# Gate logits and first convolution taps on ScalarE, and a new price list for the issue order of a hybrid conformer block

## Chip, cores and metric

One core of a Trainium2 chip. The metric is the device time of one execution in microseconds; several runs of a kernel are summed up by their median.

## What is computed

One layer (DEPTH = 1) on x of 512 tokens x 1024 channels, all in float32:

```python
x = x + 0.5 * swiglu_ffn(rms_norm(x, ffn1_norm), ffn1_w13, ffn1_w2)      # D_FF = 2816
h = rms_norm(x, mix_norm)
a, g, q, k, v, fl = split(h @ w_in)              # 512, 512, 512, 512, 512, 8 columns
u = a * sigmoid(g)                               # group A: causal depthwise conv, width 31
y_conv = silu(layer_norm(conv(u, conv_w) + conv_b))
log_f = log_sigmoid(fl + forget_b)               # group B: 8 heads x 64, forgetting attention
D = cumsum(log_f)
p = softmax(q k^T / 8 + D[t] - D[s], causal)
y_attn = p @ v
y = concat(rms_norm(y_conv), rms_norm(y_attn))
x = x + y @ w_out
x = x + 0.5 * swiglu_ffn(rms_norm(x, ffn2_norm), ffn2_w13, ffn2_w2)
out = rms_norm(x, final_norm)
```

`fl` are the gate logits, one per head and token.

## The kernel before

Activations lie with channels on the 128 partitions and 512 tokens along the free dimension, in 8 tiles `xs[d]`. A product in float32 precision is made of three fast matmuls: both operands are split into a high part (`whi`, `xh`; a ScalarE cast to fp32r) and a low part (`wlo`, `xl`; what is left, by VectorE), and `product` issues hi x hi, hi x lo and lo x hi for each of the 8 k-steps. Weights come by DMA into `raw` (three buffers); `cast` makes `whi` on ScalarE and then `wlo` on VectorE (two buffers each). Products follow one another in the order of the program (`in_turn`).

The stages are feed-forward 1 (tiles `f1...`), the mixer, and feed-forward 2 (`f2...`). In the down projections of the feed-forward stages `seven` saves an eighth of the matmuls by sums of weight blocks, made on GpSimd and VectorE. The mixer goes through `ORDER`: `c0 c1 c2 v c3 a0 a1 n a2 a3 w0 w1 w2 w3`.

- `c`: `conv_tile(i)`, 128 of the 512 convolution channels. Products `pg` and `pa`, then `u = a * sigmoid(g)`, then 31 taps. For tiles 0 and 2 a tap is a ScalarE multiplication into `tap` (two buffers) and a GpSimd sum into `acc`; for tiles 1 and 3 (`DVE_CONV`) it is one VectorE instruction on `conv`, which lies in PSUM.
- `v`: `values()`, in two halves of 260 columns: 256 of `v` and 4 gate logits, into four banks `pv` of 128 tokens each. Each bank is drained by ScalarE (`vt`, scaled by the RMS factor `rcol`) and by VectorE (`zf`, 128x4, scaled by `rcol` plus the bias). Then a chain of small VectorE instructions makes log sigmoid (`lf`) from `zf`.
- `a`: `attention(i)`, two heads: products `pq` and `pk`; `gates` (only at a0) makes the cumulative sum, which goes through DRAM (`cumd`) and comes back spread over the partitions (`ck`). For each head and block of 128 queries: scores `s` on TensorE, `sm`/`mn` on VectorE (bias and row minimum), the exponential on ScalarE, transposes `pt` on TensorE, the copy `pT` on ScalarE, and the product `po`.
- `n`: `conv_norm`, layer norm and RMS norm of the four convolution tiles, which starts when their last taps are done and ends in `yh` and `yl`.
- `w`: the output projection `wo`; w0 and w1 take the convolution half.

The order of instructions on every engine is not the order of the program text. Each call on V, S, PE, G and Q (VectorE, ScalarE, TensorE, GpSimd, the SP DMA queue) is recorded in `Plan`. `price` gives each a duration, `schedule` builds a list schedule: each operation has a rank (its urgency plus the longest path of prices behind it); at each step every engine offers the ready operation that can start first (highest rank among equals), and the earliest of these is placed. Each engine then gets its instructions in that order, and on the chip an instruction waits at the head of its queue until what it needs is there. So prices do not change what is computed, only what stands behind what. The profile gives line 242 for all of them, the line that emits.

Of the kernel before, what the change touches and what calls it, by code (L numbers as in the profile page):

```python
# [36 lines left out]
P = 128  # L37
# [22 lines left out]
ORDER = "c0 c1 c2 v c3 a0 a1 n a2 a3 w0 w1 w2 w3"  # L60
# [14 lines left out]
SEM = 0.15  # L75
COPY, ACT = 0.05, 0.07
PENALTY = 40.0
URGENT_IN, URGENT_STATS, URGENT_V, URGENT_LF, URGENT_LN, URGENT_END = 20.0, 200.0, 200.0, 200.0, 200.0, 200.0
URGENT_Q, URGENT_OUT, URGENT, URGENT_X = 3.0, 3.0, 50.0, 50.0
# [66 lines left out]
class Buf:  # L146
    def __init__(self, make, dt, slots):
        self.make, self.dt, self.slots, self.tile = make, dt, slots, None
        self.uses, self.left = [], 0
# [14 lines left out]


class Plan:


    SEM, SAME = SEM, {"V": 0.13, "S": 0.1, "G": 0.13, "PE": 0.0, "Q": 0.0}
    SWITCH = 1.3  # L170

    def __init__(self, tc):
        self.tc, self.ops, self.tags, self.joined, self.urgency = tc, [], {}, None, 0.0

    def tile(self, pool, shape, dt, tag, name, bufs=1):
        slots = self.tags.setdefault((id(pool), tag), Slots(bufs))
        buf = Buf(lambda: pool.tile(shape, dt, tag=tag, name=name, bufs=bufs), dt, slots)
        slots.queue.append(buf)
        size = int(np.prod(shape))
# [24 lines left out]
    def record(self, engine, target, method, args, kwargs):  # L204
# [30 lines left out]
        cost, table = self.price(engine, method, args, kwargs, out)  # L235
# [10 lines left out]
    def price(self, engine, method, args, kwargs, out):  # L246
# [24 lines left out]

    def schedule(self):
# [15 lines left out]
        clock = dict.fromkeys(engines, 0.0)  # L288
        ready = {e: [] for e in engines}
# [936 lines left out]
```

## Time and profile before

| | |
|---|---|
| median of 3 runs (lowest to highest) | 946.19 us (945.72 to 946.75) |
| the profiled execution | 946.2 us, span 944.5 us |
| TensorE clock granted, mean | 0.998 |
| busy, share of the span: TensorE | 932.1 us, 99% |
| weight loads | 793.7 us, 84% |
| VectorE | 653.8 us, 69% |
| ScalarE | 433.7 us, 46% |
| GpSimd | 154.0 us, 16% |
| chain that ended last | TensorE 89%, VectorE 3%, GpSimd 3%, ScalarE 3% |
| DMA | 91.19 MB, mean 97 GB/s |

The span runs from the first to the last instruction. Busy shares are means over stages that differ; a TensorE bar covers a matmul with its pipeline, so neighbouring bars overlap and a short gap between two starts leaves no idle time in this table.

### The profile page before, as it was taken

Reading aid. Unit: us, or ns where it says so; the run is one execution under the profiler, and the core shown is the slowest. Engines: PE = TensorE matmul, PEld = TensorE weight load, DVE = VectorE, ACT = ScalarE, POOL = GpSimd, SP = SyncE. Lnnn points to the kernel's source line nnn. Section 1 sums busy time; section 2 is a strip of 40 time slices with the busy share of each in tenths; the row PEclk is TensorE's granted clock in tenths of the full one; section 3 lists DMA queues with packets and bytes.
Section 4 is the critical chain, followed back from the end, with each engine's and each line's share of the span. In section 5 each row is a group of like instructions: output and inputs, shape, how many; then the busy total and the mean of one; then the engine's idle time right before and its main releaser. Section 6 shows DMA issues by size and latency. Waiting matters only on the chain.

```text
span 944.5 us, 13463 instructions
## 1 busy us (share of the span) xinstructions
PE 932.1 (99%) x5277; PEld 793.7 (84%) x5277; DVE 653.8 (69%) x990; ACT 433.7 (46%) x679; POOL 154.0 (16%) x132
## 2 busy tenths in 40 slices
PE   9999999999999999999999999999999999999997
PEld 7888999888999888897677777888899888899887
DVE  6655887657776465798977766555777755876554
ACT  7433433334433245677869755333433333433344
POOL 1000211001112000999843000000121001111000
PEclk9999999999999999999999999999999999999999
DMA  7222323232432132223211122222332222332222
GB/s 247 91 91 94 130 90 112 70 109 69 138 116 99 51 110 92 90 90 112 90 68 46 67 67 88 91 90 92 116 128 90 90 89 90 112 112 97 66 84 90
DMA packets 34207, 91.19 MB, mean 97 GB/s; under 512 B 3544, under 2 KB 13912, under 8 KB 34144
## 3 DMA queue, kind: packets, MB, share of 16 engines
q1 hardware_dynamic: 33600, 90.13, 28.4%
q8 instruction: 41, 0.67, 0.3%
q10 hardware_dynamic: 544, 0.20, 0.1%
q14 instruction: 22, 0.18, 0.1%
HBM read 88.21 MB, written 2.11 MB: 96 GB/s over the span
## 4 chain that ended last, share of the span: by engine, by line
PE 89%; DVE 3%; POOL 3%; ACT 3%; issue 1%; DMA 1%; SPq 0%; DVEq 0%; POOLq 0%
PE f2g L242 13%; PE f2u L242 13%; PE f1g L242 13%; PE f1u L242 13%; PE f1p L242 9%; PE f2p L242 9%; PE wo L242 5%; PE f2o L242 4%; PE f1o L242 3%; POOL acc L242 3%; PE pg L242 1%; PE pq L242 1%; PE pa L242 1%; PE s L242 1%; PE po L242 1%
## 5 line engine op out<-in xcount | busy, mean ns | idle before, releaser
L242 ACT CAST whi<-raw 128x1024 fp32r<-128x1024 f32 (+3 forms) x152 | 150.6, 991 | 278.8 <-issue 132.0
L242 DVE TENSOR_TENSOR wlo<-raw,whi 128x1024 fp32r<-128x1024 f32 (+3 forms) x152 | 184.8, 1216 | 21.1 <-ACT whi L242 18.3
L242 POOL TENSOR_TENSOR acc<-acc,tap 128x512 f32<-128x512 f32 x60 | 90.0, 1500 | 80.7 <-ACT tap L242 74.2
L242 PE MATMUL f1u<-xh,whi 128*128 128x512 f32 x176 | 68.8, 391 | 0.6 <-ACT xh L242 0.6
L242 PE MATMUL f1u<-xl,whi 128*128 128x512 f32 x176 | 68.6, 390 | 0.3 <-DVE xl L242 0.3
L242 PE MATMUL f2g<-xh,whi 128*128 128x512 f32 x176 | 68.7, 390 | 0.0
L242 PE MATMUL f2g<-xl,whi 128*128 128x512 f32 x176 | 68.6, 390 | 0.0
L242 PE MATMUL f2u<-xh,whi 128*128 128x512 f32 x176 | 68.6, 390 | 0.0
L242 PE MATMUL f1u<-xh,wlo 128*128 128x512 f32 x176 | 68.5, 389 | 0.0
L242 PE MATMUL f2g<-xh,wlo 128*128 128x512 f32 x176 | 68.5, 389 | 0.0
L242 PE MATMUL f2u<-xl,whi 128*128 128x512 f32 x176 | 68.5, 389 | 0.0
L242 PE MATMUL f2u<-xh,wlo 128*128 128x512 f32 x176 | 68.5, 389 | 0.0
L242 PE MATMUL f1g<-xh,whi 128*128 128x512 f32 x168 | 65.8, 392 | 0.0
L242 PE MATMUL f1g<-xl,whi 128*128 128x512 f32 x168 | 65.5, 390 | 0.0
L242 PE MATMUL f1g<-xh,wlo 128*128 128x512 f32 x168 | 65.4, 389 | 0.0
L242 POOL TENSOR_TENSOR f2S<-raw 128x512 f32<-128x512 f32 x8 | 11.1, 1392 | 310.5 <-DMA raw<-w2b 294.9
L242 DVE TENSOR_TENSOR f2un<-f2u,rstd_f2in 128x512 f32<-128x512 f32 x22 | 15.2, 691 | 63.0 <-PE f2u L242 63.0
L242 DVE TENSOR_TENSOR f1un<-f1u,rstd_in 128x512 f32<-128x512 f32 x22 | 15.2, 690 | 54.8 <-PE f1u L242 54.8
L242 POOL TENSOR_TENSOR f1S<-raw 128x512 f32<-128x512 f32 x8 | 10.4, 1294 | 261.6 <-DMA raw<-w2a 227.0
L242 ACT ACTIVATE tap<-u,par 128x512 f32<-128x512 f32 x60 | 42.8, 720 | 20.9 <-POOL acc L242 20.6
L242 DVE SCALAR_TENSOR_TENSOR conv<-u,par,conv 128x512 f32<-128x512 f32 x60 | 45.1, 752 | 1.2
L242 PEld LDWEIGHTS f1u<-xh,whi 128*128 128x128 f32 x176 | 33.1, 188 | 8.1 <-ACT xh L242 1.1
(420 smaller groups left out, 2410.3 us busy)
## 6 DMA issues: line engine op xcount, KB each, us to landing
raw<-w13b SPq DMA_DIRECT2D x44, 512.0 KB, 3.4
raw<-w13a SPq DMA_DIRECT2D x42, 512.0 KB, 3.5
raw<-w2a SPq DMA_DIRECT2D x16, 512.0 KB, 3.6
raw<-w2b SPq DMA_DIRECT2D x16, 512.0 KB, 3.5
raw<-wag SPq DMA_DIRECT2D x8, 512.0 KB, 3.4
raw<-wqk SPq DMA_DIRECT2D x8, 512.0 KB, 3.4
raw<-wo SPq DMA_DIRECT2D x8, 512.0 KB, 3.4
raw<-w2a SPq DMA_DIRECT2D x16, 192.0 KB, 2.4
```

Of the source, the lines that this page charges most:

```text
L242: ins = getattr(target, method)(*real, **kw)
```

## The change

Three things are changed; arithmetic is the same apart from where it is done.

1. The gate logits are drained by ScalarE, as `rcol` times the four columns, into `p5`, a part of the PSUM tile `ps` that is now allocated at the head of `values`; one VectorE addition of the bias for all 8 heads and 4 blocks makes `zf`.
2. The first tap of convolution tiles 1 and 3 is a ScalarE activation (as it was for tiles 0 and 2), and VectorE adds the other 30.
3. The planner has new prices and rules. Prices by form, with PSUM operands told apart; latencies between engines by the engine that was waited for; ScalarE and VectorE may start 0.1 and 0.08 us before the last instruction ends; an operation with `port` (any on GpSimd, and on VectorE a two-operand one without PSUM) does not start while the other engine has one; a change of tile size on TensorE costs 0.1 or 0.17; a DMA costs its queue 0.1 and its transfer is counted on a common bus. `URGENT`, the urgency of attention, goes from 50 to 80.

`LATE` is False, so what depends on it is as before (`ORDER`, the places of `k` and `po`); `URGENT_W` is 0.0, which changes no rank.

```diff
-SEM = 0.15
-COPY, ACT = 0.05, 0.07
+SEM = {"V": 0.05, "S": 0.05, "G": 0.05, "PE": 0.2, "Q": 2.0}
+SAME = {"V": 0.03, "S": 0.02, "G": 0.06, "PE": 0.0, "Q": 0.0}
+OVERLAP = {"V": 0.08, "S": 0.1, "G": 0.0, "PE": 0.0, "Q": 0.0}
+TILED, UNTILED = 0.1, 0.17
-URGENT_Q, URGENT_OUT, URGENT, URGENT_X = 3.0, 3.0, 50.0, 50.0
+URGENT_Q, URGENT_OUT, URGENT, URGENT_X, URGENT_W = 3.0, 3.0, 80.0, 50.0, 0.0
...
-    SEM, SAME = SEM, {"V": 0.13, "S": 0.1, "G": 0.13, "PE": 0.0, "Q": 0.0}
-    SWITCH = 1.3
+    SEM, SWITCH = 0.15, 1.3
...
         if engine == "PE":
-            dt = args[1].buf.dt
-            passes = 4 if dt == F32 and method == "matmul" else 2 if dt == F32 else 1
-            part = args[1].at[0].size / P if method == "matmul" else 1
-            return 0.003 + n * passes / 2400.0 * max(part, 0.25), None
+            if method != "matmul":
+                return n * 0.00084, None
+            part = args[1].at[0].size / P
+            if args[1].buf.dt != F32:
+                return 0.0133 + n / 2400.0, None
+            if part > 0.5:
+                return 2 * max(0.02 + n * 0.00069, 0.1), None
+            op.tiled = part
+            return (0.13 if part > 0.3 else 0.084) * max(n, 64) / P, None
         if method == "dma_start" and engine != "Q":
             return 0.1, None
+        psum = any(isinstance(v, View) and v.buf.psum for v in list(args) + list(kwargs.values()))
         if engine == "S":
+            cost = (0.143 if psum else 0.2) + n * 0.00083
             if method == "copy":
-                return COPY + n * 0.00084, None
-            return ACT + n * 0.00084, None if args[2] in (AF.Copy, AF.Square, AF.Identity) else args[2]
+                return cost, None
+            if isinstance(kwargs.get("scale"), View) or isinstance(kwargs.get("bias"), View):
+                cost += 0.09
+            if "accum_out" in kwargs:
+                op.late = 0.1
+            return cost, None if args[2] in (AF.Copy, AF.Square, AF.Identity) else args[2]
         if engine == "G":
-            return 0.1 + n * (0.0024 if method.startswith("tensor_") else 0.0012), None
+            op.port = 1.0
+            return 0.1 + n * (0.00233 if method.startswith("tensor_") else 0.0008), None
         if engine == "Q":
-            return 0.1 + n * 4 * P / 330e3, None
+            op.bytes += n * 4 * P
+            return 0.1, None
         if method == "tensor_tensor_scan":
             return 0.06 + n * 0.0022, None
         if method == "reciprocal":
-            return 0.06 + n * 0.0064, None
+            return 0.15 + n * 0.0062, None
+        if method in ("tensor_copy", "tensor_scalar") and not psum:
+            return 0.15 + n * 0.0006, None
+        if not psum:
+            op.port = 1.0
         if method == "scalar_tensor_tensor":
-            return 0.06 + n * 0.00118, None
-        return 0.06 + n * 0.00108, None
+            return 0.15 + n * 0.00118, None
+        return 0.15 + n * 0.00105, None
...
             for o in op.before.values():
-                lat = self.SAME[op.engine] if o.engine == op.engine else self.SEM
-                if o.engine == "Q":
-                    lat = 2.0
-                t = max(t, o.end + lat)
+                t = max(t, o.end + (SAME if o.engine == op.engine else SEM)[o.engine])
...
                     t = max(t, clock[e])
+                    if op.port:
+                        t = max(t, port["G" if e == "V" else "V"])
...
-            op.start, op.end = t, t + cost
-            clock[e] = op.end
+            if e == "PE" and op.tiled != tiled:
+                cost += TILED if tiled == 1.0 else UNTILED
+                tiled = op.tiled
+            op.start, op.end = t, t + cost + op.late
+            clock[e] = t + cost - (0.0 if op.late else OVERLAP[e])
+            if op.port:
+                port[e] = t + cost - (0.1 if e == "G" else 0.0)
+            if e == "Q":
+
+                bus = op.end = max(bus, t) + op.bytes / 330e3
...
-            if i in DVE_CONV and j == 0:
-                V.tensor_scalar(a, u[:, 0:T], w, bias, ALU.mult, ALU.add)
-            elif i in DVE_CONV:
+            if i in DVE_CONV and j:
                 V.scalar_tensor_tensor(a, u[:, j:j + T], w, a, ALU.mult, ALU.add)
             elif j == 0:
                 S.activation(a, u[:, 0:T], AF.Identity, scale=w, bias=bias)
...
     def values():
+
+        ps = plan.tile(pp, [P, 16, NT, H], F32, "pt", "e", PT)
+        p1, p2, p3, p4, p5 = (ps[:, n] for n in range(5))
...
-                V.scalar_tensor_tensor(zf[:, t, 4 * c:4 * c + 4], pv[t][:, 4 * HD:VC], rc,
-                                       par[:, G_FB + 4 * c:G_FB + 4 * c + 4], ALU.mult, ALU.add)
+                S.activation(p5[:, t, 4 * c:4 * c + 4], pv[t][:, 4 * HD:VC], AF.Copy, scale=rc)
             plan.urgency = 0.0
...
         plan.urgency = URGENT_LF
+        V.tensor_add(zf, p5, par[:, G_FB:G_FB + H].over(NT))
         lf, e1, e2, e3 = (tile_([P, NT, H], n, n) for n in ("lf", "e1", "e2", "e3"))
-        ps = plan.tile(pp, [P, 16, NT, H], F32, "pt", "e", PT)
-        p1, p2, p3, p4 = (ps[:, n] for n in range(4))
```

## Rows read from the trace of the kernel before

**Rows 1.** Busy time by stage: stretch, its length, each engine's busy time (instructions), clock, DMA.
```profile
17.70:362.00 344.30, 344.30 (x1844) 298.23 (x1843) 235.55 (x341) 131.20 (x189) 24.32 (x25) 1.00 0.30 100
362.00:587.00 225.00, 221.04 (x1442) 175.51 (x1441) 176.83 (x286) 156.71 (x273) 105.52 (x76) 1.00 0.24 79
587.00:932.00 345.00, 345.00 (x1883) 301.19 (x1882) 225.15 (x331) 130.14 (x189) 21.59 (x16) 1.00 0.28 94
932.00:944.50 12.50, 6.02 (x50) 5.58 (x48) 6.37 (x16) 3.29 (x9) 0.00 (x0) 0.87 0.54 168
```

**Rows 2.** Chain of waits, a product of feed-forward 2: start, length, what.
```profile
591.76 5.44 PE f2g L242 x24
```

**Rows 3.** Timeline, TensorE in the mixer: start, length, what, [idle before, its releaser].
```profile
426.38 0.50 PE L242 MATMUL pa<-xh,wlo 128*128 128x512 f32 x1 [0.58 <-DVE wlo L242]
...
452.38 0.70 PE L242 MATMUL s<-k,q 128*128 128x256 f32 x2 [1.46 <-DVE mn L242]
...
455.18 0.91 PE L242 MATMUL s<-k,q 128*128 128x384 f32 x2 [0.74 <-DVE mn L242]
...
457.57 0.40 PE L242 MATMUL pk<-xh,wlo 128*128 128x512 f32 x1
458.07 0.33 PE L242 MATMUL pt<-ident,sm 128*128 128x128 f32 x1
...
511.99 0.50 PE L242 MATMUL wo<-yl,whi 128*128 128x512 f32 x1 [0.22 <-DVE yl L242]
...
514.66 0.44 PE L242 MATMUL pt<-ident,sm 128*128 128x128 f32 x2 [0.44 <-ACT pT L242]
```

**Rows 4.** Busy time, 390 to 456 us (order: PE, PEld, DVE, ACT, POOL).
```profile
390.00:456.00 66.00, 63.09 (x370) 54.23 (x368) 61.80 (x97) 47.22 (x71) 61.28 (x41) 1.00 0.30 98
```

**Rows 5.** Timeline of VectorE in the mixer, 406 to 455 us.
```profile
406.55 0.22 DVE L242 SCALAR_TENSOR_TENSOR zf<-pv,rcol,par 128x4 f32<-128x4 f32 x1
406.68 1.51 DVE L242 TENSOR_TENSOR wlo<-raw,whi 128x1040 fp32r<-128x1040 f32 x1
...
434.58 1.22 DVE L242 TENSOR_TENSOR wlo<-raw,whi 128x1024 fp32r<-128x1024 f32 x1 [1.17 <-ACT whi L242]
435.73 0.81 DVE L242 TENSOR_SCALAR conv<-u,par 128x512 f32<-128x512 f32 x1
...
448.43 3.12 DVE L242 SCALAR_TENSOR_TENSOR conv<-u,par,conv 128x512 f32<-128x512 f32 x4
451.45 0.68 DVE L242 SCALAR_TENSOR_TENSOR q<-pq,rstd_f1n 64x512 f32<-64x512 f32 x1
452.05 0.27 DVE L242 CUSTOM_DVE_ANT_0 sm<-s,ck 128x128 f32<-128x128 f32 x1
...
452.73 2.05 DVE L242 TENSOR_TENSOR wlo<-raw,whi 128x1024 fp32r<-128x1024 f32 x1 [0.19 <-ACT whi L242]
```

**Rows 6.** The tile `tap`: instructions with their min/median/max in ns; who idled for whom.
```profile
L242 ACT ACTIVATE tap<-u,par x60: 706/724/727, 377.2 to 478.0; 128x512 f32<-128x512 f32 x60
L242 POOL TENSOR_TENSOR acc<-acc,tap x60: 1267/1295/2308, 377.9 to 478.9; 128x512 f32<-128x512 f32 x60
...
  POOL acc L242: 20.6, 24
```

**Rows 7.** Timeline of ScalarE, its smallest activations in the mixer.
```profile
425.71 0.20 ACT L242 ACTIVATE e<-e 128x32 f32<-128x32 f32 x1
425.84 0.71 ACT L242 ACTIVATE tap<-u,par 128x512 f32<-128x512 f32 x1
```

**Rows 8.** Timelines of GpSimd and VectorE, the last convolution tap on each.
```profile
478.89 2.26 POOL L242 TENSOR_TENSOR acc<-acc,tap 128x512 f32<-128x512 f32 x1 [2.66 <-ACT pT L242]
...
482.69 0.75 DVE L242 SCALAR_TENSOR_TENSOR conv<-u,par,conv 128x512 f32<-128x512 f32 x1
```

**Rows 9.** Timeline of TensorE, a product going on behind a run of small matmuls.
```profile
528.51 0.50 PE L242 MATMUL wo<-yh,whi 128*128 128x512 f32 x1
528.84 0.40 PE L242 MATMUL wo<-yl,whi 128*128 128x512 f32 x1
```

More of the change, by code (lines that the diff above doesn't have):

```diff
@@ L56 @@
 BIG = 1e30
-ORDER = "c0 c1 c2 v c3 a0 a1 n a2 a3 w0 w1 w2 w3"
+LATE = False
+ORDER = "c0 c1 c2 v c3 a0 a1 n a2 a3 w0 w1 w2 w3" if not LATE else "c0 c1 c2 v c3 a0 a1 a2 n a3 w0 w1 w2 w3"
 EARLY = 2
@@ L148, in __init__ @@
         self.make, self.dt, self.slots, self.tile = make, dt, slots, None
-        self.uses, self.left = [], 0
+        self.uses, self.left, self.psum = [], 0, False
 class Slots:
@@ L163, in __init__ @@
         self.rank, self.waits, self.start, self.end, self.follows = 0.0, 0, 0.0, None, None
+        self.port, self.tiled, self.late, self.bytes = 0.0, 1.0, 0.0, 0
 class Plan:
-    SEM, SAME = SEM, {"V": 0.13, "S": 0.1, "G": 0.13, "PE": 0.0, "Q": 0.0}
-    SWITCH = 1.3
+    SEM, SWITCH = 0.15, 1.3
     def __init__(self, tc):
-        self.tc, self.ops, self.tags, self.joined, self.urgency = tc, [], {}, None, 0.0
+        self.tc, self.ops, self.tags, self.joined, self.urgency, self.psum = tc, [], {}, None, 0.0, None
     def tile(self, pool, shape, dt, tag, name, bufs=1):
@@ L178, in tile @@
         slots.queue.append(buf)
+        buf.psum = pool is self.psum
         size = int(np.prod(shape))
@@ L234, in record @@
                     op.bufs.append(v.buf)
-        cost, table = self.price(engine, method, args, kwargs, out)
+        cost, table = self.price(op, engine, method, args, kwargs, out)
         op.cost += cost
@@ L244, in record, with price @@
         op.emits.append(emit)
-    def price(self, engine, method, args, kwargs, out):
+    def price(self, op, engine, method, args, kwargs, out):
         n = out.n if isinstance(out, View) else 512
         if engine == "PE":
-            dt = args[1].buf.dt
-            passes = 4 if dt == F32 and method == "matmul" else 2 if dt == F32 else 1
-            part = args[1].at[0].size / P if method == "matmul" else 1
-            return 0.003 + n * passes / 2400.0 * max(part, 0.25), None
+            if method != "matmul":
[7 more added lines that the diff above has]
+            return (0.13 if part > 0.3 else 0.084) * max(n, 64) / P, None
         if method == "dma_start" and engine != "Q":
             return 0.1, None
+        psum = any(isinstance(v, View) and v.buf.psum for v in list(args) + list(kwargs.values()))
         if engine == "S":
+            cost = (0.143 if psum else 0.2) + n * 0.00083
             if method == "copy":
-                return COPY + n * 0.00084, None
-            return ACT + n * 0.00084, None if args[2] in (AF.Copy, AF.Square, AF.Identity) else args[2]
+                return cost, None
[4 more added lines that the diff above has]
+            return cost, None if args[2] in (AF.Copy, AF.Square, AF.Identity) else args[2]
         if engine == "G":
-            return 0.1 + n * (0.0024 if method.startswith("tensor_") else 0.0012), None
+            op.port = 1.0
+            return 0.1 + n * (0.00233 if method.startswith("tensor_") else 0.0008), None
         if engine == "Q":
-            return 0.1 + n * 4 * P / 330e3, None
+            op.bytes += n * 4 * P
+            return 0.1, None
         if method == "tensor_tensor_scan":
@@ L288, in schedule @@
         clock = dict.fromkeys(engines, 0.0)
+        port = {"V": 0.0, "G": 0.0}
+        tiled, bus = 1.0, 0.0
         ready = {e: [] for e in engines}
@@ L375, in block_kernel @@
     pp = ctx.enter_context(tc.tile_pool(name="pp", bufs=1, space=bass.MemoryType.PSUM))
+    plan.psum = pp
     dr = ctx.enter_context(tc.tile_pool(name="dr", bufs=1, space=bass.MemoryType.DRAM))
@@ L483, in unit @@
         lo = wide(shape, "wlo", f"wlo{n}", SPLITS, F32R)
-        return cast(hi, lo, raw)
+        with plan.urgent(URGENT_W):
+            return cast(hi, lo, raw)
     def load_and_split(i, raw, hi, lo, a, b):
@@ L1031, in attention @@
             if stacked:
-                h, l = (tile_([P, T], f"u{2 * b + n}", f"k{i}{b}{n}", 1, F32R) if i % 2 == 0 else
-                        slot(16 + 2 * b + n, f"k{i}{b}{n}", F32R) for n in range(2))
+                h, l = (tile_([P, T], f"u{2 * b + n}", f"k{i}{b}{n}", 1, F32R) if (i % 2 == 0) != LATE else
+                        slot((0 if LATE else 16) + 2 * b + n, f"k{i}{b}{n}", F32R) for n in range(2))
                 G.memset(f32(l)[other], 0.0)
@@ L1049, in attention @@
         sums = tile_([P, NT, 2], "sums", f"sums{i}", 2)
-        po = bank("misc", f"po{i}", MISC) if i == 0 else bank("cv", f"po{i}")
+        po = bank("misc", f"po{i}", MISC) if i < (3 if LATE else 1) else bank("cv", f"po{i}")
         quarters = []
```

## The prediction

> **What bounds the kernel now.** I read the stages first: the busy time of each engine in stretches of the span [rows 1]. TensorE has no idle time from 587 to 932 us, nor from 18 to 362, while the middle stretch, 362 to 587 (mixer: convolution, attention, output projection), has 225.0 us with 221.0 busy. The chain of waits shows how tight the feed-forward stages are: 24 product matmuls in 5.44 us, 0.227 us each, every time [rows 2]. Nothing that VectorE, ScalarE or GpSimd do faster can shorten those stages. What can be won lies in the middle, and a little at the two ends; TensorE's granted clock is full there.
>
> A busy TensorE hides short stalls: a matmul's bar lasts 0.39 us while the next one can start after 0.227, so 0.16 of each stall lies under a bar. In the middle the timeline shows idle time before five matmuls [rows 3], at 426.38, 452.38, 455.18, 511.99 and 514.66; with 0.16 added to each they are 0.74, 1.62, 0.90, 0.38 and 0.60. Four more lie wholly under bars and are found by the starts alone, as at 457.57, where the next one comes 0.50 later in place of 0.227; they are 0.24 to 0.29 each, 1.07 together. The sum of the nine is 5.3 us. That is all there is to win in the middle without changing TensorE's own work.
>
> The next view is who the stalled matmuls wait for. The three largest name VectorE (`wlo`, then `mn` twice). VectorE is busy 61.8 of the 66 us from 390 to 456, GpSimd 61.3, ScalarE only 47.2 [rows 4]. VectorE's timeline at the largest stall shows its queue: four convolution taps of 3.12 us, then `q`, then the `sm` whose `mn` frees the score bank [rows 5]. VectorE ran its list without a gap and was simply late. One reason is in the same view: the cast's second half `wlo` took 1.22 us with GpSimd out of its way and 2.05 beside a tap sum; the tap sum on GpSimd took 1.27 to 2.31, median 1.295 [rows 5, 6]. The old planner prices neither.
>
> **The change, part by part.** *VectorE gets lighter.* Two first taps leave, 0.81 us each, one of them at 435.73 [rows 5]: 1.6 us. Eight `zf` instructions leave; one is 0.22 us long but the next instruction starts 0.13 after it [rows 5], so 8 x 0.13 = 1.0 (1.7 at the full length). One add of 128x32 comes back, between 0.13 and 0.22. Net: 2.4 us off, 3.1 at most, all before 450 us, in the stretch where VectorE has 4.2 us of idle.
>
> *ScalarE gets heavier.* Two taps at 0.72 [rows 6], 1.3 to 1.4 us with the overlap of neighbours. Eight copies of four columns: no row shows one; the nearest is a 32-column `e` of 0.20 us [rows 7], so 0.1 (overlapped) to 0.2 each, I take 0.15, since the tap behind that `e` starts 0.13 after it: 1.2. Together 2.5 us (2.1 to 3.0) on an engine with 18.8 us idle in that stretch. What hides it is that idle; without that cover the cast `whi` behind the copies is late, then `wlo`, then the product that needs it, up to 1.6 us at the second group of gate columns.
>
> The Trainium skill, page ScalarE: Activation LUTs, section Rules for kernel authors, speaks against this move: it wants adds and multiplications on VectorE, not on ScalarE. No sentence of the sum uses it; here the f32 tap takes 0.72 on ScalarE and 0.81 on VectorE [rows 5, 6], so the trace does not agree for this form.
>
> *The order.* Nothing on TensorE is added or removed. The planner's price of a 512-column ScalarE tap rises from 0.50 to 0.72 (0.62 after overlap), which is what the row says [rows 6]; the price of three product matmuls from 0.65 to 0.68, as in the chain; a sum of two SBUF operands on VectorE and any GpSimd instruction are now planned one after the other. DMA issues no longer hold the queue for their transfer: in the plan small transfers (the row sums' detour through DRAM, `cumd` and `ck`) may go earlier, never behind a load's transfer; the real queue has the same waits for freed buffers as before. The wait that the change adds is one: `zf` now follows a ScalarE copy and one add. Queued behind that add on VectorE are convolution taps; who needs it (the transposes of `lf`) is over 5 us later behind a whole product, so I cost it at nothing, and at 0.4 us if that cover were gone.
>
> *What that is worth at the nine places.* At 452 and 455 (2.52): VectorE arrives 2.4 us earlier less what falls into its idle time; I take 2.0. At 426 (0.74): `wlo` has less ahead of it, but its `whi` now stands behind more on ScalarE; I take 0, with 0.74 and -1.6 as bounds. At 512 and 515 (0.98): the wait is for `yl`, the end of the chain that starts when the last convolution tap is done. The last tap on VectorE starts at 482.69, after GpSimd's last at 478.89 [rows 8], so a lighter VectorE brings this forward; I take half, 0.5. The four smaller ones (1.07): a better price of ScalarE helps them in general; 0.3, bounds 0 and 1.07. What is late next at 452 would be ScalarE's `sm` and the cast behind its taps, which is why I don't take all. Sum: 2.0 + 0 + 0.5 + 0.3 = 2.8.
>
> *Both ends.* From 932 on the order of small steps is replanned too; with the same operations I expect 0, bounds 0.5 either way. The head waits for transfers of x and weights, which do not change.
>
> The profiled execution has a span of 944.5 us and a time of 946.2, so 1.7 lie around the span; the median of the runs is 946.19, the same. Forecast: 946.2 - 2.8 = **943.4**.
>
> **Rivals.**
> 1. *More and smaller batches on TensorE.* Between 362 and 587 I count 53 runs of small matmuls (scores, transposes, sums) between product matmuls. After one, the first product matmul takes 0.33 us in place of 0.227, as at 528.51 [rows 9]; with the change into it I price a run at 0.1 to 0.2, 0.15 as a middle. The prices of switching lengthen the plan but choose nothing. With each score ready at its own time, and attention's urgency up from 50 to 80, runs may split: 16 more cost 2.4 us: 943.4 + 2.4 = 945.8, no change. For it: ScalarE is now planned slower, so pieces are ready further apart. Against: fewer late pieces also means fewer splits around a stall.
>    The Trainium skill, page TensorEngine Tiling (Array Packing), section Key Properties, says that a change of tiling mode drains TensorE. By it only the runs of 32 and 64 columns would pay; the 0.10 at 528.51, behind a 64-column run, agrees.
> 2. *ScalarE takes the place of VectorE.* Taps on ScalarE wait for GpSimd 24 times, 20.6 us in all [rows 6], and everything behind a waiting tap waits too. If the eight copies stand ahead of the casts between 410 and 430, the stall at 426 grows by up to 1.6, and 0.6 is lost at the next cast: 943.4 + 2.2 = 945.6. Against: ScalarE has 28% of the stretch idle.
> 3. *The convolution ends later: slower.* In the plan a tap sum and a `wlo` now stand apart: 1.295 + 1.22 = 2.52 us; overlapped the longer of the two needed 2.05 to 2.31 [rows 5, 6]. If the plan opens a gap on GpSimd for each of some 20 casts before 480 us, at 0.35 (2.52 less a middle of 2.17), the taps end 7.0 us later. GpSimd's last tap starts 3.8 us before VectorE's last but lasts 1.5 longer, so 2.3 are slack; beyond that the wait for `yl` at 512, which has no slack left, grows one for one: 4.7. With the 2.0 won at 452 and 455: 946.2 - 2.0 + 4.7 = 948.9. It is slower by more than the bound from about 18 such gaps. Against: 2.4 us come off VectorE, and a tap sum that waits in the plan waits on the chip as well.
>    The Trainium skill, page SBUF — State Buffer, section Who interferes with whom, says that the second of two such instructions blocks fully until the first is done. By it standing apart costs next to nothing and this rival is void; the 2.05 to 2.31 seen here lie just under the 2.52 of full blocking, so the trace leans to it.
> 4. *The order hardly changes* where it matters; then only the ten moved instructions count, half of the gain: 944.8.
>
> **How the numbers follow.** Forecast 0.58; rival 1 0.15; rival 2 0.10; rival 3 0.12; rival 4 0.05. About 0.2%, 1.9 us, is what a measurement of this kernel can tell from no change, so faster means under 944.3 and slower over 948.1: faster 0.58, same 0.15 + 0.10 + 0.05 = 0.30, slower 0.12. Low end: all nine places gone and 0.5 at the tail, 946.2 - 5.3 - 0.5 = 940.4. High end: it takes in rivals 1, 2 and 4 and the mild half of rival 3 (some 16 gaps): 946.2 - 2.0 + 16 x 0.35 - 2.3 = 947.5. What lies outside is about 1 in 10 above and less below, as the nine places limit the gain.
>
> **What would show it.** Right: busy TensorE from 362 to the start of the second feed-forward stage, with that stretch shorter by about 2.8 us; both feed-forward stages unchanged at 5.44 us per 24; VectorE under 60 us in the 66 from 390; no wait of a score matmul for `mn` over 0.5 us; eight ScalarE copies of 128x4 at 0.2 or less. Rival 1 shows as over 65 runs of small matmuls; rival 2 as TensorE waiting for `wlo` with `whi` just before it on ScalarE; rival 3 as the last tap after 486 us and a wait for `yl` of several us. The forecast is wrong if TensorE's idle time merely moves to other places in the middle, or if the head or the feed-forward stages show stalls that they do not have now.

## The result and the profile after

The changed kernel takes 949.23 us (median of 6 runs, 947.31 to 950.38), the kernel before 946.09 beside it (945.66 to 946.79): a ratio of 1.003, interval 1.002 to 1.004. It is **slower by 0.3%**, where 943.4 was forecast. The profiled execution of after took 949.7 us with a span of 947.9, so the tables of the two traces differ by 3.4 us of span.

The page of after, its span and busy times:

```profile
span 947.9 us, 13474 instructions
PE 933.5 (98%) x5277; PEld 796.3 (84%) x5277; DVE 653.1 (69%) x981; ACT 434.5 (46%) x688; POOL 154.6 (16%) x132
```

The stretches of after, with the columns of [rows 1] and [rows 4] (length, then busy us and instructions of PE, PEld, DVE, ACT and POOL, granted clock, DMA share, GB/s). The first and the last are the feed-forward stages:

```profile
17.70:362.00 344.30, 344.30 (x1845) 298.55 (x1845) 234.46 (x342) 131.18 (x188) 25.41 (x25) 1.00 0.30 100
390.00:456.00 66.00, 60.62 (x355) 53.21 (x354) 56.47 (x87) 43.95 (x75) 50.69 (x34) 0.97 0.29 97
...
587.00:932.00 345.00, 345.00 (x1875) 300.77 (x1872) 225.66 (x330) 130.94 (x188) 22.35 (x16) 1.00 0.28 94
```

The feed-forward stages have no idle time, as before. In the 66 us from 390, VectorE went from 61.8 to 56.5 us, as the change meant it to, though by more than the 2.4 us that were taken off it: over the whole span VectorE is busy 653.1 us where it was 653.8, so part of its work only stands later. GpSimd went from 61.3 to 50.7. But TensorE is busy for only 60.6 of these 66, and the granted clock has a mean of 0.97. All but 0.2 us of the loss lies in the middle: the second feed-forward stage begins its matmuls at 582.41 where it began at 579.13, 3.28 us later, and goes on at the pace of [rows 2]. The chain of before at that place, then the chain of after, its first and a later link there:

```profile
579.13 3.41 PE f2g L242 x15
```

```profile
582.41 4.08 PE f2g L248 x18
...
595.03 5.44 PE f2g L248 x24
```

What TensorE waited for from 362 to 587 in after, the first three (us in total, times, longest):

```profile
PE pv L248 <- DVE wlo L248: 4.4, 2, 3.0
PE s L248 <- DVE mn L248: 0.7, 2, 0.5
PE s L248 <- DVE k L248: 0.5, 1, 0.5
```

The wait of scores for `mn`, the largest before, went from 2.2 to 0.7, and those of `pa` for `wlo` and of `wo` for `yl` are not in the list any more [rows 3]. In their place stand two waits in the product of the values, where before only one matmul began late, by 0.2 us at 408.24. TensorE's timeline of after (start, length, idle before it and who ended it):

```profile
409.59 0.39 PE L248 MATMUL pv<-wlo,xh 128*128 128x260 f32 x1 [1.39 <-DVE wlo L248]
...
418.67 0.39 PE L248 MATMUL pv<-wlo,xh 128*128 128x260 f32 x1 [3.04 <-DVE wlo L248]
...
419.74 0.42 PE L248 MATMUL pv<-whi,xh 128*128 128x260 f32 x1
419.95 0.42 PE L248 MATMUL pv<-wlo,xh 128*128 128x260 f32 x1
```

With the part hidden under the bars, counted as for [rows 3] by the starts, they are 1.55 and 3.20 us: 4.75. And one microsecond after the second, the value matmuls go from 0.12 us apart to 0.215: TensorE has fallen to its lower level, 1.2 GHz, and stays there until 423.18. Its clock in that stretch (length, PE busy, granted clock, DMA share, GB/s):

```profile
415.60:418.60 3.00, 0.03 (x1) 1.00 0.00 0
419.80:423.00 3.20, 3.20 (x17) 0.50 0.36 140
```

3.4 us at half speed lose 1.7. **The account of the middle** is then as follows. The late starts (the times by which matmuls of the middle begin later than the pace allows, as summed for [rows 3]) are 5.36 us before and 7.38 after. Of the 7.38, 4.75 are new; the rest, 2.63, is 2.7 less than before, about the gain that was forecast (2.8). 7.38 - 5.36 + 1.7 = 3.7; the stretch is longer by 3.3, and the 0.4 between are about what three runs of small matmuls fewer (50 where there were 53) are worth at 0.1 each [rows 9].

**Why was `wlo` late?** Its first half was not: ScalarE's timeline of after ends the two `whi` at 405.00 and 410.67, 2.9 and 5.8 us before the `wlo` made from them begins.

```profile
403.96 1.04 ACT L248 CAST whi<-raw 128x1040 fp32r<-128x1040 f32 x1
...
409.61 1.06 ACT L248 CAST whi<-raw 128x1040 fp32r<-128x1040 f32 x1
```

VectorE's timeline of after shows what it did with those microseconds:

```profile
402.51 5.49 DVE L248 SCALAR_TENSOR_TENSOR conv<-u,par,conv 128x512 f32<-128x512 f32 x7
407.91 1.62 DVE L248 TENSOR_TENSOR wlo<-raw,whi 128x1040 fp32r<-128x1040 f32 x1
409.46 7.08 DVE L248 SCALAR_TENSOR_TENSOR conv<-u,par,conv 128x512 f32<-128x512 f32 x9
416.45 2.17 DVE L248 TENSOR_TENSOR wlo<-raw,whi 128x1040 fp32r<-128x1040 f32 x1
418.54 3.12 DVE L248 SCALAR_TENSOR_TENSOR conv<-u,par,conv 128x512 f32<-128x512 f32 x4
...
427.34 0.19 DVE L248 TENSOR_TENSOR zf<-e,par 128x32 f32<-128x32 f32 x1 [4.56 <-ACT e L248]
```

Seven taps and then nine, for which no matmul waits here, run ahead of the two casts that TensorE stands still for; a little later VectorE is idle for 4.56 us. Before, the first of the two began at 406.68 [rows 5] and the second at 412.06, as VectorE's timeline of before shows:

```profile
412.06 1.24 DVE L242 TENSOR_TENSOR wlo<-raw,whi 128x1040 fp32r<-128x1040 f32 x1
```

The planner chose the new order. GpSimd's timeline of after shows why it could: nine tap sums in one block.

```profile
405.77 13.98 POOL L248 TENSOR_TENSOR acc<-acc,tap 128x512 f32<-128x512 f32 x9 [0.27 <-ACT e L248]
```

The new rule raises the earliest start of an operation with `port` to the end of the other engine's, and then the planner takes the operation with the earliest start:

```python
if op.port:
    t = max(t, port["G" if e == "V" else "V"])
...
key = (t, -rank, op.index)
if pick is None or key < pick[0]:
    pick = (key, t, op)
```

`wlo` reads two SBUF operands, so it has the port and can start only when GpSimd's sum ends; a VectorE tap works on `conv` in PSUM, has no port, and can always start at once. As long as GpSimd has its next sum ready and VectorE a tap, the tap wins whatever the ranks are. That is the theory tested below (**the port chooses**, theory A in the expectations). Its rivals: the port's durations themselves are at fault; the moved instructions on ScalarE are (theory B); the other new prices or the urgency of 80 are (theory C); or the casts don't matter, since VectorE has a fixed amount to do before the first scores and a wait removed in one place comes back in the next (**the wait moves on**, theory D).

### The profile page after: what moved, and what is told of

Its sections match the earlier page's. It is cut to its first block, busy times and chain, and to the rows that moved or that the text cites. A ratio compares the mean times of both kernels' runs of the same rounds, so it can differ in the third digit from the quotient of the medians.

```text
span 947.9 us, 13474 instructions
## 1 busy us (share of the span) xinstructions
PE 933.5 (98%) x5277; PEld 796.3 (84%) x5277; DVE 653.1 (69%) x981; ACT 434.5 (46%) x688; POOL 154.6 (16%) x132
## 4 chain that ended last, share of the span: by engine, by line
PE 90%; DVE 5%; ACT 3%; issue 1%; DMA 1%; SPq 0%; DVEq 0%
PE f2g L248 13%; PE f2u L248 13%; PE f1u L248 13%; PE f1g L248 13%; PE f2p L248 9%; PE f1p L248 9%; PE wo L248 5%; PE f2o L248 4%; PE f1o L248 3%; DVE conv L248 3%; PE pg L248 2%; PE pa L248 2%; DVE wlo L248 2%; PE s L248 2%; PE pq L248 1%
## 5 line engine op out<-in xcount | busy, mean ns | idle before, releaser
L248 POOL TENSOR_TENSOR f2S<-raw 128x512 f32<-128x512 f32 x8 | 10.4, 1297 | 310.4 <-DMA raw<-w2b 278.4
L248 POOL TENSOR_TENSOR f1S<-raw 128x512 f32<-128x512 f32 x8 | 10.4, 1295 | 260.2 <-DMA raw<-w2a 225.5
```

What stands on the lines that cost most here:

```text
L248: ins = getattr(target, method)(*real, **kw)
```

## The experiments

Each was timed beside the kernel before. A ratio is to that kernel on the same chip, with its 95% interval; its medians were 946.2 to 946.6.

### The rule taken away, and the rule kept out of the choice

```diff
 # no_port
-                    if op.port:
-                        t = max(t, port["G" if e == "V" else "V"])
```

> The changed kernel without the two lines that hold VectorE and GpSimd apart in the plan; the moved work, the new prices and the urgency stay. Theory A (the port rule starves the cast): in the changed kernel the `wlo` of the last two gate/value weights stand behind 7 and 9 convolution taps, which need no port and can always start sooner in the plan; TensorE waits 1.55 and 3.20 us for them and its clock is then at half for 3.4 us (1.6 lost). Without the rule 5 and 6 taps stand there: both waits under 1 us each, no drop of the clock, 943 to 945 us. Theory B (the moved work: the copies of the gate logits delay `whi` on ScalarE): the waits stay, 948 to 950. Theory C (the other prices or the urgency of 80): the waits stay, 948 to 950.

Measured 954.2 (953.58 to 955.86), 1.0086 (1.0072 to 1.01): far slower. The value products wait less, but new waits stand elsewhere. TensorE's waits from 362 to 600, the first three, and the instruction of VectorE's timeline that makes `k`, which the first scores read:

```profile
PE s L248 <- POOL acc L248: 2.6, 1, 2.6
PE pv L248 <- DVE wlo L248: 1.1, 1, 1.1
PE ssq_conv L248 <- POOL sq_conv L248: 1.0, 1, 1.0
...
450.75 0.69 DVE L248 TENSOR_TENSOR k<-pk,rstd_f1n 128x512 f32<-128x512 f32 x1
```

The first line puts the wait of the scores down to GpSimd's `acc`. But that sum ended at 451.59, and the matmul had begun at 451.58; `k` ended at 451.44, 0.14 us ahead of the matmul, much as in after (450.04 and 450.19). So it is VectorE that comes late there, and GpSimd at `sq_conv`. The late starts add up to 10.4 us, and the two feed-forward stages are longer than in after by 0.9 and 0.8. A likely reason, not tested, is that a plan in which `wlo` and the tap sums overlap freely doesn't hold on the chip: its four `wlo` of 128x1040 took 1.64 to 2.10 us where the plan had priced 1.24 (0.15 + 1040 x 0.00105). So the rule can't just be dropped, and 943 to 945 was a miss. The next kernel keeps it as a delay and leaves it out of the comparison:

```diff
 # port_no_choice
-                    if op.port:
-                        t = max(t, port["G" if e == "V" else "V"])
...
                     if pick is None or key < pick[0]:
+                        if op.port:
+                            t = max(t, port["G" if e == "V" else "V"])
                         pick = (key, t, op)
```

> The changed kernel with the port still counted for when an instruction starts in the plan, but no longer for which instruction an engine takes next: a cast with the higher rank is taken and waits for the port. Theory A: it is the choice that does the harm and not the port's durations, so this behaves as without the rule: waits at the value products under 1 us each, 943 to 945 us. Theory B and theory C: 948 to 950. If the durations of the port themselves spoil the plan (taps late, as rival 3 of the prediction had it): over 946 with the waits elsewhere.

Measured 946.21 (945.94 to 946.77), ratio 1.0 (0.9991 to 1.0009): the loss is gone, 3.0 us to the changed kernel's 949.23. VectorE's timeline of this kernel, then TensorE's at the one value product that still waits:

```profile
402.81 3.91 DVE L248 SCALAR_TENSOR_TENSOR conv<-u,par,conv 128x512 f32<-128x512 f32 x5
406.63 1.83 DVE L248 TENSOR_TENSOR wlo<-raw,whi 128x1040 fp32r<-128x1040 f32 x1
408.38 5.49 DVE L248 SCALAR_TENSOR_TENSOR conv<-u,par,conv 128x512 f32<-128x512 f32 x7
413.78 1.23 DVE L248 TENSOR_TENSOR wlo<-raw,whi 128x1040 fp32r<-128x1040 f32 x1
...
415.07 0.39 PE L248 MATMUL pv<-wlo,xh 128*128 128x260 f32 x1 [0.52 <-DVE wlo L248]
```

Five and seven taps in place of seven and nine, 0.7 us of wait in place of 4.75. The same prices, the same moved work: only what the port does to the choice differs. Yet the sum of late starts is 5.67, about that of before: waits at `pq` (0.9), for `k` (0.7) and for `mn` (0.9) stand where the gain should have been, and at 512 to 516 some 2 us for GpSimd's `sq_conv` and for `yl`.

### The two halves of the change, each alone

```diff
 # moves_only: the kernel before, with the moved work alone
-            if i in DVE_CONV and j == 0:
-                V.tensor_scalar(a, u[:, 0:T], w, bias, ALU.mult, ALU.add)
-            elif i in DVE_CONV:
+            if i in DVE_CONV and j:
...
-                V.scalar_tensor_tensor(zf[:, t, 4 * c:4 * c + 4], pv[t][:, 4 * HD:VC], rc, ...)
+                S.activation(p5[:, t, 4 * c:4 * c + 4], pv[t][:, 4 * HD:VC], AF.Copy, scale=rc)
...
+        V.tensor_add(zf, p5, par[:, G_FB:G_FB + H].over(NT))
```

> The kernel before with the gate logits and the first taps on ScalarE and nothing else: the old planner. Theory A: no starving, VectorE 2.4 us lighter; waits for `mn` at the first attention tile (2.5 us in the kernel before) shrink: 943.5 to 945.5 us. Theory B: a wait for `wlo` at the value products of 3 us or more, 948 to 950. Theory C has nothing to say against 943.5 to 945.5.

Measured 947.2 (944.77 to 949.21), 1.0008 (0.9999 to 1.0017): no gain. Its waits (the largest), VectorE's timeline at that wait, and the stretch of [rows 4] in this kernel:

```profile
PE s L242 <- DVE mn L242: 2.0, 1, 2.0
...
448.11 3.12 DVE L242 SCALAR_TENSOR_TENSOR conv<-u,par,conv 128x512 f32<-128x512 f32 x4
...
390.00:456.00 66.00, 63.42 (x367) 55.27 (x366) 62.71 (x92) 49.56 (x83) 60.19 (x41) 0.97 0.32 103
```

This run fells a step of the prediction. VectorE lost the instructions that the prediction took off, and yet four taps still stand ahead of the first `sm`, the stall at 450 still costs 2.15 us by the starts, and VectorE is as busy up to 456 as before: the stretch holds 43 convolution instructions in both kernels, though two first taps have left it, so the planner filled the room with taps that were to come later. Counted from the mixer's first matmul, `k` ends 1.3 us earlier than before, but the first `mn` no earlier. The instant at which `mn` comes is set by what the planner puts ahead of it, not by the sum of VectorE's work. That the time didn't fall has two more reasons in the trace: a stall of 1.7 us at 513, where `wo` waits for `wlo`, and 3.4 us at half clock behind the stall at 450, which is the 0.97 of the last row.

```diff
 # planner_only: the changed kernel, with the moved work put back on VectorE
-            if i in DVE_CONV and j:
+            if i in DVE_CONV and j == 0:
+                V.tensor_scalar(a, u[:, 0:T], w, bias, ALU.mult, ALU.add)
+            elif i in DVE_CONV:
...
-                S.activation(p5[:, t, 4 * c:4 * c + 4], pv[t][:, 4 * HD:VC], AF.Copy, scale=rc)
+                V.scalar_tensor_tensor(zf[:, t, 4 * c:4 * c + 4], pv[t][:, 4 * HD:VC], rc, ...)
...
-        V.tensor_add(zf, p5, par[:, G_FB:G_FB + H].over(NT))
```

> The changed kernel with the gate logits and the first taps back on VectorE: the new planner alone. Theory A: the last two `wlo` of the value weights again stand behind 6 taps with four gate logits, and 7 to 9 taps: waits of 1.5 us and over 2 us there, 947 to 951. Theory B: without the copies on ScalarE no such wait, 944 to 946. Theory C: as theory A in time; told apart by the run without the port rule.

Measured 945.9 (945.22 to 946.81), 0.9994 (0.9985 to 1.0003): same, where 947 to 951 was expected. The planner alone, then, doesn't lose. In its VectorE timeline the `zf` instructions break up the run of taps, and the second `wlo` comes at 413.51 in place of 416.45:

```profile
408.02 1.62 DVE L248 TENSOR_TENSOR wlo<-raw,whi 128x1040 fp32r<-128x1040 f32 x1
...
412.06 1.54 DVE L248 SCALAR_TENSOR_TENSOR conv<-u,par,conv 128x512 f32<-128x512 f32 x2
413.51 1.24 DVE L248 TENSOR_TENSOR wlo<-raw,whi 128x1040 fp32r<-128x1040 f32 x1
```

The first starved cast is there (1.54 us of wait), the second isn't; the largest wait is for `k` at the first scores, 2.05 us by the starts. The larger of the two value waits is there in the changed kernel and in neither half alone (0.67 in moves_only), so it needs both: the rule and, as it seems, a VectorE that has nothing but taps left to choose. That was not in my theory, which had put it all on the planner.

### The two casts issued earlier, nothing else moved

```diff
 # value_casts_first: in the finished order, each wlo of the values goes ahead of the taps
 # that the plan starts after its whi is there
+        for op in [o for o in order if o in self.first]:
+            i = order.index(op)
...
+            ready = max(o.end + (SAME if o.engine == "V" else SEM)[o.engine] for o in op.before.values())
+            at = i
+            for n in range(i - 1, floor, -1):
+                if order[n].engine == "V":
+                    if order[n] not in self.taps or order[n].start < ready:
+                        break
+                    at = n
+            order.insert(at, order.pop(i))
...
```

> The changed kernel with one edit behind the planner: the `wlo` of the last two value weights are issued two and four convolution taps earlier on VectorE (5 and 7 taps ahead of them in place of 7 and 9); every other instruction on every engine keeps its place. Theory A (these two places are the whole loss): the waits of TensorE at the value products shrink from 1.55 and 3.20 us to under 1 us in all, the clock stays up, and the time falls from 949.2 to 943.5 to 945 us, below the kernel before. Theory D (the time only moves on, because VectorE has no spare time and the taps now come later): 947 to 949.

> The changed kernel as it is, beside the others on one chip: 947.3 to 950.4 us, with the granted clock lower in the longer runs if the half clock sets the spread.

Two places in VectorE's order change: the casts stand behind 5 and 7 taps in place of 7 and 9. Measured 946.24 (945.21 to 946.42), 0.9997 (0.9989 to 1.0006); the changed kernel on the same chip 949.39 (948.71 to 950.99), 1.0032 (1.002 to 1.0044). Two instructions in other places are worth 3.1 us, the whole loss. This and port_no_choice show the cause: **those two casts behind too many taps**. But 4.0 us of the value waits went (0.7 stays), and the half clock with them; of these more than 5 us only 3.1 came back. Where the rest stayed (TensorE's timeline of this kernel):

```profile
413.96 0.39 PE L252 MATMUL pv<-wlo,xh 128*128 128x260 f32 x1 [0.55 <-DVE wlo L252]
...
421.68 0.50 PE L252 MATMUL pg<-xh,wlo 128*128 128x512 f32 x1 [1.36 <-DVE wlo L252]
```

The next cast, behind eight taps, is now late by 1.5 us.

### Does the half clock come from the idle time, and what does it cost

```diff
 # fill: ahead of the two waiting matmuls, products into a bank that nobody reads
+                        for n in range((6, 13)[kh] if c == 1 and t == 0 and k == 0 else 0):
...
+                            PE.matmul(fill, xh[0][:, :P], xh[0], start=True, stop=True)
...
```

> The changed kernel with 6 and 13 extra matmuls of 128x512 on TensorE (1.36 and 2.95 us, into an unused bank) right before the two waits for `wlo`; all other orders are the same, so the waiting times stay but TensorE is busy in them. If the half clock of 3.4 us comes from the idle time before it: no drop of the clock, all runs within 1 us, 947.0 to 947.6 us. If it does not: 948 to 950 with a spread of 3 us, as the changed kernel.

Measured 948.01 (947.46 to 950.26), 1.0018 (1.0009 to 1.0027), 1.4 us under the changed kernel of the same chip. The stretches of this kernel that answer to those of after, with the same columns:

```profile
415.60:418.60 3.00, 3.00 (x16) 1.00 0.00 0
419.80:423.00 3.20, 3.20 (x29) 1.00 0.53 169
```

The order on all engines is that of the changed kernel and the casts come just as late, but TensorE has something to do meanwhile and the clock stays full. So the half clock follows the idle time, and is worth 1.4 of the 3.1 us.

### Urgency put back

```diff
 # urgent_50
-URGENT_Q, URGENT_OUT, URGENT, URGENT_X, URGENT_W = 3.0, 3.0, 80.0, 50.0, 0.0
+URGENT_Q, URGENT_OUT, URGENT, URGENT_X, URGENT_W = 3.0, 3.0, 50.0, 50.0, 0.0
```

> The changed kernel with attention's urgency back at 50. In its VectorE order four taps and a `q` stand ahead of the first `sm` again, as in the kernel before. Theory A: the waits at the value products stay as in the changed kernel (4.75 us, and the clock), and if it was the urgency that took the wait for `mn` away, it is back at 1.5 to 2.5 us: 950 to 952 us. If the lighter VectorE took it away: 948 to 950 and no such wait. Theory C (the urgency makes the loss): 944 to 947.

Measured 951.7 (949.82 to 952.58), 1.0054 (1.0041 to 1.0066): 2.3 us slower than the changed kernel. The value waits are the same to a tenth; part of what comes back is the wait of the scores for `mn`. Two of its waits, and VectorE's timeline at the first scores:

```profile
PE pv L248 <- DVE wlo L248: 4.4, 2, 3.1
PE s L248 <- DVE mn L248: 1.3, 2, 0.8
...
452.25 3.12 DVE L248 SCALAR_TENSOR_TENSOR conv<-u,par,conv 128x512 f32<-128x512 f32 x4
455.28 0.67 DVE L248 SCALAR_TENSOR_TENSOR q<-pq,rstd_f1n 64x512 f32<-64x512 f32 x1
455.88 0.27 DVE L248 CUSTOM_DVE_ANT_0 sm<-s,ck 128x128 f32<-128x128 f32 x1
```

Four taps, `q`, `sm`: the very order of [rows 5], with VectorE lightened. So it is the urgency that decides whether taps stand ahead of the first `sm`. It doesn't show that the urgency won the 1.3 us at the first scores: with it back at 50 the stall there is 1.1 us by the starts, no more than the 1.28 of after (0.65 for `k`, 0.63 for `mn`), as TensorE comes to them 4.5 us later than before. The larger part of the loss stands behind: the waits of the output projection from 514 to 527, for `sq_conv`, `yl` and `pT`, are 2.4 us where after has 0.9. Theory C, that the urgency makes the loss, falls: without it the kernel is slower still, and the other new prices stand in port_no_choice too, which doesn't lose.

### Every late cast pulled forward: does anything come of it

If the cause is starvation, freeing all casts should bring 2 us more; if the wait moves on, it should not.

```diff
 # casts_first: as value_casts_first, for the wlo of every product
...
-        with plan.urgent(URGENT_W):
-            return cast(hi, lo, raw)
+        w = cast(hi, lo, raw)
+        plan.first.append(plan.ops[-1])
+        return w
 # casts_first_slack: a cast may also go ahead of a tap that starts up to 1.5 us before its whi is there
-                    if order[n] not in self.taps or order[n].start < ready:
+                    if order[n] not in self.taps or order[n].start < ready - 1.5:
 # casts_k_first: casts_first_slack, and the same for k
+        plan.first.append(plan.ops[-1])
```

> As the run with the value casts first, and the next `wlo` (of the fourth convolution tile's first weight) three taps earlier too, behind 5 taps in place of 8: the moving of value casts alone had left a wait of 1.53 us there and 0.71 at the last value weight. Theory A: the 1.53 goes, 944.5 to 945.2 us. Theory D (VectorE has no spare time, the wait moves on): 946 to 947.

> The same, with every product's `wlo` of the mixer let ahead of taps that the plan starts up to 1.5 us before the cast's high half is done in the plan (one more tap ahead in most places). Theory A: the 0.71 goes too, 944.0 to 945 us. If VectorE now waits for `whi` with taps behind it: 945 to 947.

> The same as the run with slack, and `k` (scaled keys, for which TensorE waits 0.88 us before the first scores) let ahead of taps as well. Theory A: 943.5 to 944.5 us. If the wait is then for `ck` or `mn` (the next to be late): as the run with slack.

Measured 947.72 (946.35 to 948.99), 1.001 (1.0001 to 1.0019); 947.37 (946.5 to 949.41), 1.0011 (1.0002 to 1.002); 947.13 (946.53 to 947.39), 1.0005 (0.9996 to 1.0014). None gains; the first two are a little slower than the kernel before. In casts_first the 1.5 us at `pg` are gone, and `pq` (1.3 us) and the first scores wait in their place. TensorE's timeline of casts_first at the first scores and ScalarE's 25 us earlier, then TensorE's waits in casts_k_first:

```profile
447.93 0.46 PE L252 MATMUL s<-k,q 128*128 128x128 f32 x2 [1.85 <-DVE k L252]
...
422.25 0.59 ACT L252 COPY acc<-conv 128x512 f32<-128x512 f32 x1 [2.09 <-DVE conv L252]
```

```profile
PE s L252 <- DVE k L252: 1.1, 1, 1.1
PE pq L252 <- DVE wlo L252: 1.1, 1, 1.1
```

`k` began at 444.98 in value_casts_first and at 447.09 here; 1.1 of these 2.1 us is only that the whole mixer begins later in this execution. The other microsecond goes by ScalarE: the taps that the cast overtook end later, ScalarE stands 2.09 us for the last of them (1.07 in value_casts_first), and the last copies of the gate logits, `zf` and all that VectorE does between them and `k` move back with it. With `k` pulled forward too, its wait falls from 2.0 to 1.2 by the starts and `mn` is late by 0.7. Here the rival holds: up to the first scores each wait that is taken away comes back at a later place. The half clock has a part in the times too: in the profiles of casts_first and casts_first_slack TensorE runs 3.4 us at half speed behind the wait for `k`, in that of casts_k_first it doesn't.

```diff
 # planner_no_choice: the two edits of port_no_choice, and those of planner_only, as
+                V.tensor_scalar(a, u[:, 0:T], w, bias, ALU.mult, ALU.add)
...
-        V.tensor_add(zf, p5, par[:, G_FB:G_FB + H].over(NT))
```

> The new planner with the port counted for the start but not for the choice, and the gate logits and first taps back on VectorE: against the run port_no_choice (946.2 us) it tells what the moved work is worth under a planner that does not starve the casts, against planner_only (945.9) what the choice by port costs when the moved work stays on VectorE. Theory A: the wait of 1.54 us at the third value weight goes, 944.3 to 945.5 us. If lighter VectorE is worth its 2.4 us under this planner: 948 to 949. Theory D (VectorE is the limit up to the first scores and a wait that goes comes back later): 945.5 to 946.5.

Measured 946.07 (945.15 to 947.49), 0.9997 (0.9988 to 1.0007), against 946.21 with the moved work. Under a plan without starvation, ten instructions fewer on VectorE bring nothing that can be measured; the first `k` ends at 446.66 without them and at 446.80 with them, and the times agree although the profile with them has 3.4 us at half clock from 447.5, which the other has not. No kernel of this study beats the one before by more than the measurement can tell; planner_only is the lowest, by 0.06%.

## Why the prediction was wrong

The side was wrong and the range missed: 949.2 lies above 947.5.

**The step that failed first: the order.** The prediction went through the new prices one by one, said of the port that `wlo` and the tap sums were "now planned one after the other", and gave it no term in the sum. It didn't put two things together that both stood in the kernel: the planner takes the earliest start before it looks at the rank, and the port makes an earliest start later for some VectorE instructions and not for others. A rule that is true as a duration thus became a preference for taps. [Rows 4] and [rows 5] had all that was needed: GpSimd busy with tap sums nearly without pause, a VectorE with taps always at hand, and casts that TensorE waits for. What it cost: 4.75 us of new waits and 1.4 of lost clock, against 2.7 won.

**The step that failed second: "VectorE arrives 2.4 us earlier".** moves_only has the lighter VectorE and keeps the stall at 450; urgent_50 has it too, with the new prices, and again has four taps ahead of the first `sm`; between port_no_choice and planner_no_choice the lighter VectorE moves `k` by 0.1 us. In an order that a planner refills, time taken off an engine need not arrive at a given instruction: it is filled from behind, or comes back as idle. From the second convolution tile's `u` to the first `k`, VectorE was busy 56.1 us and idle 3.9 before, 53.4 and 9.5 after. The terms, by the late starts of the two traces:

| place | forecast gain | before | after | gain |
|---|---|---|---|---|
| first scores, 452 and 455 | 2.0 | 2.55 | 1.28 | 1.27 |
| `pa`, 426 | 0 | 0.74 | none | 0.74 |
| 512 and 515 | 0.5 | 0.99 | 0.90 | 0.09 |
| four smaller ones | 0.3 | 1.08 | 0.45 | 0.63 |
| product of the values | none | none | 4.75 | -4.75 |

The first four add to 2.7 for 2.8, but no term has its size, and the first hasn't its reason; that the sum fits is chance. Nor did VectorE arrive earlier: the first `mn` ends at 452.89 where it ended at 452.33. The stall behind it is shorter (0.63 for 1.63) because TensorE, held up by the value waits, is ready for that matmul at 452.3 where it was at 450.7; the gain is in part the other side of the loss. At 515 the prediction also misread its rows: the second stall there waits for `pT` on ScalarE, not for `yl`, before and after alike.

**ScalarE's part** was about as sized. The eight copies of 128x4, by shape, in after (count, busy us, mean ns, then idle before them):

```profile
L248 ACT ACTIVATE e<-pv,rcol 128x4 f32<-128x4 f32 x8 | 1.8, 228 | 4.8 <-PE pv L248 4.8
```

0.23 each where 0.2 was the limit set, with the next instruction 0.14 to 0.16 after the start of each (0.15 was taken), and no matmul waits for them: **rival 2** falls, since `whi` was done long before `wlo` began. **The wait that the change adds** cost nothing, as priced: `zf` stands 4.56 us at the head of VectorE's queue, but the cast behind it got its `whi` only at 427.18, 0.16 before `zf` began. The taps that the prediction saw queued behind it were not there: all thirty of that tile had been taken by 421.7. **Rival 1** falls: 50 runs of small matmuls, not 65. Its last sentence read too much into one row: in before a first product matmul takes 0.31 us behind a run of 128 columns too (531.34), so the 0.10 does not point to the change of tiling. **Rival 4** falls too: the order changed where it matters.

**Rival 3** came near in size (948.9) and in its side, and stood on the same rule, but its mechanism is another. Its gaps did open: GpSimd is 10.6 us less busy in [rows 4]'s stretch, and its last tap begins at 489.9 where it began at 478.9 [rows 8]. No wait for `yl` followed. It asked what the rule does to GpSimd, and the harm was done to VectorE, on the other side of it. The conclusion drawn there from the Trainium skill (page SBUF — State Buffer, section Who interferes with whom), that standing apart costs next to nothing, is about the chip's time and says nothing of what a plan does with the rule. For the chip itself the rows hardly differ: `wlo` took 1.22 to 2.17 us in after from 407 to 428, 1.22 to 2.05 before [rows 5]. One of these rows the prediction misread: the `wlo` of 1.22 us at 434.58 did not have GpSimd out of its way, as GpSimd's timeline of before shows:

```profile
434.65 2.31 POOL L242 TENSOR_TENSOR acc<-acc,tap 128x512 f32<-128x512 f32 x1
```

In that pair `wlo` began first and kept its pace, and the sum took 2.31 us; in the pair of 452.73 the sum began first, at 452.44, and took 1.27, and `wlo` took 2.05.

**What held:** both feed-forward stages unchanged; VectorE at 56.5 in the stretch, under the 60 set; no wait for `mn` over 0.5 (in part by luck, since TensorE came later); the sentence on what would make it wrong, idle time that moves within the middle.

**Open:** why no_port loses so much more than the waits it saves was located (`k` on VectorE and `sq_conv` on GpSimd late, and the feed-forward stages longer) but not tested; nor was what a full replanning with the port as a true shared resource would give.

## What to carry to other kernels

A list scheduler that picks by earliest start turns every availability rule into a priority: before adding one, ask which instructions it doesn't touch, for these will always be taken first. When an edit takes work off an engine whose order is planned, read its gain from where that engine's critical instruction lands in the new order, not from the busy time saved. And where engines have a fixed amount to do before a stage can begin, pulling one late instruction forward can move the wait to a later one, by way of another engine's queue too; count all waits up to that stage, not the one that is cured.

## What the hardware showed that was not expected

TensorE fell to 1.2 GHz after 3.04 us of idle in a stretch where it had been busy nearly throughout, 1.1 us after it had taken up work again, and that cost 1.4 us in the median. In the profile of changed_again, with the same order and 3.07 us of idle, it fell at 417.6, while it still stood idle, and stayed low for 6.8 us in place of 3.4. It isn't tied to the length of the idle alone: moves_only fell after the 2.0 us stall at 450, as the granted clock of its two stretches there shows, and casts_first after 1.85 us of idle, while planner_only kept the full clock across 1.89 us, no_port across 2.59, and the kernel before across the stalls at 452 and 455 [rows 3]. Why it falls in one and not in another was not settled.

```profile
450.00:451.90 1.90, 0.09 (x1) 1.00 0.45 181
...
452.50:455.70 3.20, 3.20 (x10) 0.50 0.30 97
```

The changed kernel's executions differ in this too: 947.31 us at a mean clock of 0.998, 950.38 at 0.993. So the stall of 3.04 us cost about half as much again as it lasted, by the medians, and not alike in every execution.
